# Side loads of the HGRN2 heads and the attention on another queue, in other tiles and in smaller portions

## The chip, the cores and the metric

The kernel runs on one core of a Trainium2 chip. The metric is the device time of one execution in microseconds. An execution is profiled separately, and its trace gives the rows below. Engines: TensorE (PE; its weight loads are PEld), VectorE (DVE), ScalarE (ACT), GpSimd (POOL) and SyncE (SP), which only issues transfers; "q" behind an engine's name is its queue. Each engine takes its instructions in the order of its queue.

## The reference, cut to what matters

A decoder of two layers on x of 1024 rows and 1024 columns, all in float32:

```python
mod = c_act @ ada_w[l] + ada_b[l]                  # 6 vectors of 1024 a layer, 2 more for keys and values
sh1, sc1, g1, sh2, sc2, g2 = jnp.split(mod, 6, axis=-1)
h = modulate(x, sh1, sc1)                          # RMS norm, scale, shift
y = hgrn2_mixer(h, ...)   # layer 0: 8 heads of 128: proj = h @ w_in gives q, f, i, g; chunked scan
y = fox_mixer(h, ...)     # layer 1: 8 heads of attention with forget gates, keys and values shared
x = x + g1 * y
h = modulate(x, sh2, sc2)
u = causal_conv3(h @ w_up)                         # 2 x 2816 channels
x = x + g2 * ((silu(gate) * val) @ w_down)
```

## The kernel before

Each product is of float32 precision: an operand is split into a rounded high part (ScalarE, line 83) and the rest (VectorE, line 84), and three matmuls (lines 102 to 104) add up. Weights come as 512 KB transfers issued by SP into one of two raw buffers (`wraw`); the split goes to one of three buffers (`whl`). The MLP's products are done with block sums of operands and weights, so that seven half-size products stand for eight; for w_down the kernel first forms sums of its rows (`weight_sums`) and stores them in DRAM (`sd`), from where `ffn_down` loads them.

The stages in order are `start` (norm and first modulation), `hgrn` (eight heads), `mixer_out`, `ffn_up`, `ffn_down`, `shared_kv`, `fox` (eight heads of attention), and again `mixer_out`, `ffn_up` and `ffn_down`.

Heads are counted from 0: head 2 is the third. A head of `hgrn` is `forget` (dense product, sigmoid at line 618, cumulative sums, exponentials), `rest` (three dense products for q, i and g), `scan` (transposes, a product masked by VectorE's copy at line 697, the state products at line 710 and the recurrence at line 719) and `outputs`, with `gate` one head later. `gate` puts the head's output in a stream tile. There are eight stream tiles (`x_tile`, pool `xp`); in the heads they are free once x is spilled to DRAM in head 0, and are taken up one by one by the outputs.

Beside the heads runs side work. `ada_plan` makes a list of steps, one for each 128 rows of an adaLN vector's weights: load 512 KB (line 301, GpSimd's queue, one of three buffers `raw`) and multiply and add into `acc` (VectorE, line 305 for the first and 307 for the other seven). When a vector's eight steps are done, `ada_close` sums over partitions with matmuls (line 353). `weight_sums` makes eleven pairs of row blocks of w_down, each with two loads (line 330), one sum and three differences of half rows (lines 331 and 336) and two stores (line 339). For layer 0 a pair is one step of the same list, with the same three buffers, behind the first 48 adaLN steps; 48 more follow it. `ada_step(n)` takes n steps from the list: `SIDE` says how many behind q, behind i and behind the scan. For layer 1 the sums run in `fox`, two steps of 44 at each query block, in stream tiles.

In `ffn_up`, group j makes 128 gate and 128 value channels; `weight_tiles(j)` loads its two raw weights (line 825) into `wraw`, and `weights` splits them and their block sums. `first_groups` does groups 0 and 1 together and begins group 2, while `flush` still makes the operands from the eight stream tiles. The framework sets the order on each queue and the waits when it builds the program; a buffer's next user waits for its last reader.

Of the kernel before, what the change touches and what calls it, by code (L numbers as in the profile page):

```python
# [4 lines left out]
F32 = mybir.dt.float32  # L5
# [8 lines left out]
P = 128  # L14
D = 1024
S = 1024
# [30 lines left out]
ST = 1  # L47
NAT = (5, 0)
KLATE = True
SIDE = (4, 6, 4)  # L50
LATE = 7
FILL = ((1, 1, 1), (2, 0, 2), (2, 0, 2), (0, 2, 3), (2, 0, 2), (2, 1, 4), (0, 0, 1), (2, 0, 2))

# [1 line left out]
class Trunk:  # L55
# [240 lines left out]
    def ada_plan(self, vectors):  # L296

        def block(key, v, one, k, box):
            def step():
                raw = self.adap.tile([P, D], F32, tag="raw", name="ada_raw", bufs=3)  # L300
                self.nc.gpsimd.dma_start(raw, self.ada_w[key][k * P:(k + 1) * P, v * D:(v + 1) * D])
                c = self.cact[:, k:k + 1]
                if k == 0:
                    box.append(self.adap.tile([P, D], F32, tag="acc", name="acc", bufs=1))
                    self.nc.vector.tensor_scalar(out=box[0], in0=raw, scalar1=c, scalar2=None, op0=ALU.mult)
                else:
                    self.nc.vector.scalar_tensor_tensor(out=box[0], in0=raw, scalar=c, in1=box[0],  # L307
                                                        op0=ALU.mult, op1=ALU.add)
                if k == KT - 1:
                    self.ada_open.append((key, v, one, box[0]))  # L310
            return step

        for key, v, one in vectors:
            box = []
            self.ada_todo += [block(key, v, one, k, box) for k in range(KT)]

    def weight_sums(self, l, tiles):

        V, G, down = self.nc.vector, self.nc.gpsimd, self.t["ffn_w_down"][l]

        def pair(i):
            e, o = [], []

            def first():
                for r, raws in ((2 * i, e), (2 * i + 1, o)):
                    raws.append(tiles())
                    G.dma_start(raws[0], down[r * P:(r + 1) * P, :])  # L330
                V.tensor_tensor(out=o[0][:, HALF:D], in0=e[0][:, HALF:D], in1=o[0][:, HALF:D], op=ALU.add)

            def minus(out, a, b, row=None, raws=None):
                def f():
                    (t0, c0), (t1, c1), (t2, c2) = out, a, b
                    V.tensor_tensor(out=t0[0][:, c0:c0 + HALF], in0=t1[0][:, c1:c1 + HALF], in1=t2[0][:, c2:c2 + HALF],
                                    op=ALU.subtract)
                    if raws:
                        G.dma_start(self.sd[l][row * P:(row + 1) * P, :], raws[0])
                return f  # L340

            return [first, minus((e, HALF), (e, 0), (e, HALF)), minus((e, 0), (o, HALF), (e, 0), 2 * i, e),
                    minus((o, 0), (o, 0), (e, 0), 2 * i + 1, o)]

        return [pair(i) for i in range(NFF // 2)]

    def ada_close(self):

        nc = self.nc
        for key, v, one, acc in self.ada_open:  # L350
            ps = self.aux_tile()
            for j in range(KT):
                nc.tensor.matmul(ps[:, j:j + 1], acc[:, j * P:(j + 1) * P], self.ones[:, 0:1], start=True, stop=True)
            s = slice(v * KT, (v + 1) * KT)
            dst, bias = self.mods[key][:, s], self.ada_bias[key][:, s]
            if one:
                nc.vector.scalar_tensor_tensor(out=dst, in0=ps[:, 0:KT], scalar=1.0, in1=bias, op0=ALU.add, op1=ALU.add)
            else:
                nc.vector.tensor_tensor(out=dst, in0=ps[:, 0:KT], in1=bias, op=ALU.add)
        self.ada_open = []  # L360

    def ada_step(self, n):

        todo, self.ada_todo = self.ada_todo[:n], self.ada_todo[n:]
        for step in todo:
            step()
# [220 lines left out]
    def hgrn(self, hs):  # L587
# [3 lines left out]
        with self.work("hg") as wp:  # L591
            def T(tag):
                return wp.tile([P, S], F32, tag=tag, name="hg_" + tag)
# [47 lines left out]
                return a, b, c, d, e  # L641

            def rest(h, a, b, c, d, e, before):
                pq = self.mm_tile()
                w = self.early.pop(0) if self.early else self.w_cols(w_in, h * P)
                for n in range(2):
                    self.dense(pq[:, n * HALF:(n + 1) * HALF], w, hs, n)
                    if n == 0:
                        self.ada_close()
                q = T("q")  # L650
                nc.scalar.activation(q, pq, AF.Silu)
                nc.vector.tensor_tensor(out=e, in0=q, in1=e, op=ALU.mult)
                nc.vector.tensor_tensor(out=q, in0=q, in1=c, op=ALU.mult)
                self.ada_step(SIDE[0])

                pi = self.mm_tile()
                w = self.w_cols(w_in, 2 * D + h * P)
                for n in range(2):
                    self.dense(pi[:, n * HALF:(n + 1) * HALF], w, hs, n)
                    if n == 0:  # L660
                        self.ada_close()
                before()
                vt = T("a")
                nc.scalar.copy(vt, pi)
                self.ada_step(SIDE[1])

                pg = self.mm_tile()
                w = self.w_cols(w_in, 3 * D + h * P)
                for n in range(2):
                    self.dense(pg[:, n * HALF:(n + 1) * HALF], w, hs, n)  # L670
                    if n == 0:
                        self.ada_close()
                sg = T("sg")
                nc.scalar.activation(sg, pg, AF.Silu)
                self.ada_close()

                return b, c, d, e, q, vt, sg
# [90 lines left out]
            f, before = forget(0), lambda: None  # L768
            for h in range(NH):
                b, c, d, e, q, vt, sg = rest(h, *f, before)  # L770
                if h == 0:
                    for n in range(2):
                        self.spill_x(n)
                v, sv = scan(b, c, d, e, q, vt)
                if h == 0:
                    self.conv_setup()
                self.ada_step(SIDE[2])
                if h < NH - 1:
                    f = forget(h + 1)
                before = lambda h=h, on=outputs(q, v, sv), sg=sg: gate(h, on, sg)  # L780
# [34 lines left out]
    def ffn_up(self, l, ops):  # L815


        nc, t, V = self.nc, self.t, self.nc.vector
# [1 line left out]
        Q = KT // 2  # L820

        def weight_tiles(j):
            g, v = (self.wraw.tile([P, S], F32, tag="wraw", name="wraw_t") for _ in range(2))
            for raw, c0 in ((g, j * P), (v, (NFF + j) * P)):
                nc.sync.dma_start(raw.rearrange("p (k m) -> p k m", k=KT),
                                  up[:, c0:c0 + P].rearrange("(k p) m -> p k m", p=P))
            return g, v
# [99 lines left out]
        def first_groups():  # L927
# [14 lines left out]
            gate_right(a)  # L942
            first_gate(b)
            raws = weight_tiles(2)
            do(p7(a))
            do(p4(a))
# [329 lines left out]
    def fox(self, hs):  # L1276
        nc, t = self.nc, self.t
        wq = t["b_w_q"][0]
        V, G = nc.vector, nc.gpsimd
        self.ogf = [None] * NH  # L1280
        with self.work("fx") as wp:
# [36 lines left out]
            def head_sig(s):  # L1318
                s["sg"] = wp.tile([P, S], F32, tag="sg", name="fx_sg")
                with self.tc.high_priority():  # L1320
                    nc.scalar.activation(s["sg"], s["pg"], AF.Sigmoid)
                    self.ln_exp_set()
# [75 lines left out]
            norm()  # L1398
            advance(s, 16)
            head_sig(s)  # L1400
            sums = [f for steps in self.weight_sums(1, lambda: self.x_tile("down_raw")[0]) for f in steps]
            for h in range(NH):
                last = h == NH - 1
                for i in range(KT):
                    if h < 3 or i < 4:
                        for f in sums[:2]:
                            f()
                        sums = sums[2:]
                    ls = logits(s, i)
                    if not last:  # L1410
                        if i == 0:
# [51 lines left out]
    def body(self):  # L1463
        t, mod = self.t, self.mod

        def new():
            return [[None, None] for _ in range(KT)]

        h, hk, h1 = new(), new(), new()
        self.sqacc = [None, None]  # L1470
        self.pending = []
        self.ada_todo, self.ada_open = [], []
        with self.work("ln") as self.lnp, self.work("first") as wp:
            self.start(wp, h)
        self.ada_plan([(0, v, v == 4) for v in (2, 3, 4, 5)] + [("kv", v, v == 1) for v in range(2)])
        self.ada_todo += [lambda steps=steps: [f() for f in steps] for steps in self.weight_sums(0, lambda: self.adap.tile([P, D], F32, tag="raw", name="down_raw", bufs=3))]
        self.ada_plan([(1, v, v in (1, 4)) for v in range(6)])

        def ln(hs, shift, scale1, keep=False):
# [63 lines left out]
```

## Time and profile before

| | |
|---|---|
| median of 3 runs | 2630.34 us (2621.69 to 2631.52) |
| profiled execution | 2626.53 us, span 2624.8 us |
| mean granted TensorE clock | 0.977 |
| busy TensorE, VectorE, ScalarE, GpSimd | 96%, 71%, 46%, 12% of the span |
| moved by DMA | 362.11 MB, mean 138 GB/s |

The span goes from the first to the last instruction. A row of windows has the stretch (us from the span's start), its length, the busy us (and count) of PE, PEld, DVE, ACT and POOL, the granted clock, the mean busy share of the 16 DMA engines, and GB/s; with a line or tile given, the busy us are those of its instructions on the engines that have any. The granted clock is a share of full speed. Busy time of TensorE is modelled, since its matmuls are pipelined. A row of waits names who waited, for whom, for how long in total, how often, and the longest.

### The profile page before, as it was taken

What the parts mean: (1) busy time and instruction counts of PE and PEld (TensorE: products, weight loads), DVE (VectorE), ACT (ScalarE), POOL (GpSimd) and SP (SyncE); (2) the same over time, 40 slices, a digit from 0 to 9 for tenths busy, and PEclk for the clock granted to TensorE, in tenths of its full rate; (3) what the DMA queues carried; (4) which work ended last, traced back from release to release, by engine and by line L of the source; (5) the groups of instructions that cost most, each with busy time, mean ns of one, the idle gap of its engine ahead of it and who ended that gap; (6) DMA issues with size and microseconds to landing.
All of it is one profiled execution on the core that took longest, in us unless ns stands there. A gap on an engine that the chain in (4) does not pass through costs nothing.

```text
span 2624.8 us, 32311 instructions
## 1 busy us (share of the span) xinstructions
PE 2529.3 (96%) x12312; PEld 2089.2 (80%) x12312; DVE 1859.0 (71%) x2703; ACT 1204.2 (46%) x1767; POOL 325.0 (12%) x464
## 2 busy tenths in 40 slices
PE   7999988999999999999999999999998999999999
PEld 5788777778778888878888987888886887887887
DVE  6666656675877878886765367767658777879754
ACT  6333222234544444544645355556545444445442
POOL 3212222211000000000120034323210000000000
PEclk8999998899999999999999999999999999999999
DMA  8653667535122222573343457432511222228423
GB/s 291 193 161 97 209 208 249 161 111 165 37 81 80 82 87 81 177 258 111 125 138 125 149 209 273 148 101 73 165 61 57 80 86 75 81 89 296 137 94 119
DMA packets 298642, 362.11 MB, mean 138 GB/s; under 512 B 14166, under 2 KB 214980, under 8 KB 298486
## 3 DMA queue, kind: packets, MB, share of 16 engines
q1 hardware_dynamic: 271510, 263.30, 30.7%
q0 software_dynamic: 26976, 96.73, 10.7%
q8 instruction: 97, 1.59, 0.2%
q14 instruction: 59, 0.48, 0.1%
HBM read 276.06 MB, written 83.92 MB: 137 GB/s over the span
## 4 chain that ended last, share of the span: by engine, by line
PE 70%; DVE 11%; DMA 8%; issue 6%; ACT 2%; POOL 1%; SPq 0%; POOLq 0%; DVEq 0%; ACTq 0%
PE mm_t L102 12%; PE mm_t L104 12%; PE mm_t L103 12%; PE aux_t L102 10%; PE aux_t L104 10%; PE aux_t L103 10%; DMA ada_raw<-in_ada_w 3%; DMA wraw_t<-in_ffn_w_up 2%; DVE whl_t L84 2%; DMA sd<-down_raw 1%; PE aux_t L1369 1%; DMA down_raw<-in_ffn_w_down 1%; DVE op_t L84 1%; DVE acc L307 1%; ACT whl_t L83 1%
## 5 line engine op out<-in xcount | busy, mean ns | idle before, releaser
L84 DVE TENSOR_TENSOR whl_t<-wraw_t,whl_t 128x1024 fp32r<-128x1024 f32 (+1 forms) x332 | 374.7, 1139 | 124.7 <-ACT whl_t L83 120.8
L83 ACT CAST whl_t<-wraw_t 128x1024 fp32r<-128x1024 f32 (+1 forms) x332 | 320.1, 975 | 281.1 <-DVE wraw_t L842 91.9
L102 PE MATMUL mm_t<-op_t,whl_t 128*128 128x512 f32 x968 | 379.1, 393 | 15.4 <-ACT whl_t L83 11.6
L103 PE MATMUL mm_t<-op_t,whl_t 128*128 128x512 f32 x968 | 378.7, 392 | 1.9 <-DVE op_t L84 1.9
L104 PE MATMUL mm_t<-op_t,whl_t 128*128 128x512 f32 x968 | 377.9, 391 | 0.0
L102 PE MATMUL mm_t<-h_t,whl_t 128*128 128x512 f32 x896 | 365.5, 408 | 0.0
L103 PE MATMUL mm_t<-h_t,whl_t 128*128 128x512 f32 x896 | 356.5, 398 | 1.2 <-DVE h_t L446 0.9
L102 PE MATMUL aux_t<-op_t,whl_t 128*128 128x512 f32 x880 | 349.7, 398 | 7.2 <-ACT whl_t L83 4.1
L104 PE MATMUL mm_t<-h_t,whl_t 128*128 128x512 f32 x896 | 356.4, 398 | 0.0
L103 PE MATMUL aux_t<-op_t,whl_t 128*128 128x512 f32 x880 | 344.4, 391 | 1.2 <-DVE op_t L84 1.1
L104 PE MATMUL aux_t<-op_t,whl_t 128*128 128x512 f32 x880 | 342.9, 391 | 2.4 <-DVE whl_t L84 2.4
L102 PEld LDWEIGHTS mm_t<-op_t,whl_t 128*128 128x128 f32 x968 | 182.6, 189 | 58.8 <-ACT whl_t L83 13.3
L103 PEld LDWEIGHTS mm_t<-op_t,whl_t 128*128 128x128 f32 x968 | 182.8, 189 | 41.3 <-DVE op_t L84 4.2
L104 PEld LDWEIGHTS mm_t<-op_t,whl_t 128*128 128x128 f32 x968 | 182.5, 189 | 39.3 <-DVE whl_t L84 1.4
L102 PEld LDWEIGHTS aux_t<-op_t,whl_t 128*128 128x128 f32 x880 | 165.7, 188 | 54.5 <-ACT whl_t L83 15.5
L104 PEld LDWEIGHTS mm_t<-h_t,whl_t 128*128 128x128 f32 x896 | 171.9, 192 | 38.0 <-issue 0.5
L103 PEld LDWEIGHTS mm_t<-h_t,whl_t 128*128 128x128 f32 x896 | 172.5, 193 | 34.7 <-DVE h_t L446 1.3
L102 PEld LDWEIGHTS mm_t<-h_t,whl_t 128*128 128x128 f32 x896 | 172.3, 192 | 33.7 <-issue 2.1
L104 PEld LDWEIGHTS aux_t<-op_t,whl_t 128*128 128x128 f32 x880 | 165.3, 188 | 38.8 <-DVE whl_t L84 3.3
L103 PEld LDWEIGHTS aux_t<-op_t,whl_t 128*128 128x128 f32 x880 | 165.7, 188 | 37.0 <-DVE op_t L84 2.9
L403 POOL TENSOR_TENSOR sqacc<-sqacc,sq 128x512 f32<-128x512 f32 x29 | 43.2, 1489 | 765.6 <-ACT sq L402 765.2
L307 DVE SCALAR_TENSOR_TENSOR acc<-ada_raw,cact,acc 128x1024 f32<-128x1024 f32 x84 | 107.6, 1281 | 38.0 <-DMA ada_raw<-in_ada_w 33.5
(317 smaller groups left out, 4395.9 us busy)
## 6 DMA issues: line engine op xcount, KB each, us to landing
wraw_t<-in_ffn_w_up SPq DMA_DIRECT2D x88, 512.0 KB, 3.8
ada_raw<-in_ada_w POOLq DMA_DIRECT2D x80, 512.0 KB, 4.9
down_raw<-in_ffn_w_down POOLq DMA_DIRECT2D x44, 512.0 KB, 5.5
sd<-down_raw POOLq DMA_DIRECT2D x44, 512.0 KB, 4.1
gd<-u SPq DMA_DIRECT2D x44, 512.0 KB, 2.6
graw<-gd SPq DMA_DIRECT2D x44, 512.0 KB, 6.4
wraw_t<-sd SPq DMA_DIRECT2D x40, 512.0 KB, 3.4
wraw_t<-in_a_w_in SPq DMA_DIRECT2D x32, 512.0 KB, 5.2
```

Of the source, the lines that this page charges most:

```text
L83: self.nc.scalar.copy(hi, src)
L84: self.nc.vector.tensor_tensor(out=lo, in0=src, in1=hi.bitcast(F32), op=ALU.subtract)
L102: mm(out, wh, xh, start=start, stop=False, skip_group_check=onto)
L103: mm(out, wh, xl, start=False, stop=False, skip_group_check=onto)
L104: mm(out, wl, xh, start=False, stop=stop, skip_group_check=onto)
L307: self.nc.vector.scalar_tensor_tensor(out=box[0], in0=raw, scalar=c, in1=box[0], op0=ALU.mult, op1=ALU.add)
L403: (nc.gpsimd if k in SQPOOL else nc.vector).tensor_tensor(out=self.sqacc[n], in0=self.sqacc[n], in1=sq, op=ALU.add)
L1369: nc.tensor.transpose(pp[:, b * P:(b + 1) * P], ls[:, kb * P:(kb + 1) * P], self.ident)
```

## The change

- The transfers of the adaLN steps and of the sums (loads and stores) are issued by SP instead of GpSimd.
- The sums of layer 0 leave the list of adaLN steps: `sum_step(4)` takes one pair's four steps, once in head 0 behind the scan, and in heads 1 to 5 behind q and behind i. Their tiles are stream tiles.
- While `ada_spare` is set (from the end of head 0 until the scan of head 5), every second adaLN load has a stream tile instead of one of the three buffers.
- `SIDE` has four portions: 2 steps at the start of `rest`, 3 behind q, 4 behind i and 3 behind the scan, 12 a head for 96 steps.
- In `ffn_up`, the raw weights of group 2 go to two stream tiles instead of `wraw`, in both layers.

```diff
@@ -47,7 +47,7 @@
 ST = 1
 NAT = (5, 0)
 KLATE = True
-SIDE = (4, 6, 4)
+SIDE = (3, 4, 2, 3)
 LATE = 7
 FILL = ((1, 1, 1), (2, 0, 2), (2, 0, 2), (0, 2, 3), (2, 0, 2), (2, 1, 4), (0, 0, 1), (2, 0, 2))
 
@@ -297,8 +297,12 @@
 
         def block(key, v, one, k, box):
             def step():
-                raw = self.adap.tile([P, D], F32, tag="raw", name="ada_raw", bufs=3)
-                self.nc.gpsimd.dma_start(raw, self.ada_w[key][k * P:(k + 1) * P, v * D:(v + 1) * D])
+                self.ada_turn += 1
+                if self.ada_spare and self.ada_turn % 2:
+                    raw = self.x_tile("ada_raw")[0]
+                else:
+                    raw = self.adap.tile([P, D], F32, tag="raw", name="ada_raw", bufs=3)
+                self.nc.sync.dma_start(raw, self.ada_w[key][k * P:(k + 1) * P, v * D:(v + 1) * D])
                 c = self.cact[:, k:k + 1]
                 if k == 0:
                     box.append(self.adap.tile([P, D], F32, tag="acc", name="acc", bufs=1))
@@ -319,7 +323,7 @@
 
 
 
-        V, G, down = self.nc.vector, self.nc.gpsimd, self.t["ffn_w_down"][l]
+        V, G, down = self.nc.vector, self.nc.sync, self.t["ffn_w_down"][l]
 
         def pair(i):
             e, o = [], []
@@ -358,6 +362,12 @@
             else:
                 nc.vector.tensor_tensor(out=dst, in0=ps[:, 0:KT], in1=bias, op=ALU.add)
         self.ada_open = []
+
+    def sum_step(self, n=4):
+
+        todo, self.sums = self.sums[:n], self.sums[n:]
+        for step in todo:
+            step()
 
     def ada_step(self, n):
 
@@ -641,6 +651,7 @@
                 return a, b, c, d, e
 
             def rest(h, a, b, c, d, e, before):
+                self.ada_step(SIDE[2])
                 pq = self.mm_tile()
                 w = self.early.pop(0) if self.early else self.w_cols(w_in, h * P)
                 for n in range(2):
@@ -652,6 +663,8 @@
                 nc.vector.tensor_tensor(out=e, in0=q, in1=e, op=ALU.mult)
                 nc.vector.tensor_tensor(out=q, in0=q, in1=c, op=ALU.mult)
                 self.ada_step(SIDE[0])
+                if 0 < h < 6:
+                    self.sum_step()
 
                 pi = self.mm_tile()
                 w = self.w_cols(w_in, 2 * D + h * P)
@@ -663,6 +676,8 @@
                 vt = T("a")
                 nc.scalar.copy(vt, pi)
                 self.ada_step(SIDE[1])
+                if 0 < h < 6:
+                    self.sum_step()
 
                 pg = self.mm_tile()
                 w = self.w_cols(w_in, 3 * D + h * P)
@@ -771,10 +786,14 @@
                 if h == 0:
                     for n in range(2):
                         self.spill_x(n)
+                    self.ada_spare = True
+                if h == 5:
+                    self.ada_spare = False
                 v, sv = scan(b, c, d, e, q, vt)
                 if h == 0:
                     self.conv_setup()
-                self.ada_step(SIDE[2])
+                    self.sum_step()
+                self.ada_step(SIDE[3])
                 if h < NH - 1:
                     f = forget(h + 1)
                 before = lambda h=h, on=outputs(q, v, sv), sg=sg: gate(h, on, sg)
@@ -820,7 +839,8 @@
         Q = KT // 2
 
         def weight_tiles(j):
-            g, v = (self.wraw.tile([P, S], F32, tag="wraw", name="wraw_t") for _ in range(2))
+            g, v = (self.x_tile("uraw")[0] if j == 2 else self.wraw.tile([P, S], F32, tag="wraw", name="wraw_t")
+                    for _ in range(2))
             for raw, c0 in ((g, j * P), (v, (NFF + j) * P)):
                 nc.sync.dma_start(raw.rearrange("p (k m) -> p k m", k=KT),
                                   up[:, c0:c0 + P].rearrange("(k p) m -> p k m", p=P))
@@ -1398,14 +1418,12 @@
             norm()
             advance(s, 16)
             head_sig(s)
-            sums = [f for steps in self.weight_sums(1, lambda: self.x_tile("down_raw")[0]) for f in steps]
+            self.sums = [f for steps in self.weight_sums(1, lambda: self.x_tile("down_raw")[0]) for f in steps]
             for h in range(NH):
                 last = h == NH - 1
                 for i in range(KT):
                     if h < 3 or i < 4:
-                        for f in sums[:2]:
-                            f()
-                        sums = sums[2:]
+                        self.sum_step(2)
                     ls = logits(s, i)
                     if not last:
                         if i == 0:
@@ -1469,11 +1487,11 @@
         h, hk, h1 = new(), new(), new()
         self.sqacc = [None, None]
         self.pending = []
-        self.ada_todo, self.ada_open = [], []
+        self.ada_todo, self.ada_open, self.ada_turn, self.ada_spare = [], [], 0, False
         with self.work("ln") as self.lnp, self.work("first") as wp:
             self.start(wp, h)
         self.ada_plan([(0, v, v == 4) for v in (2, 3, 4, 5)] + [("kv", v, v == 1) for v in range(2)])
-        self.ada_todo += [lambda steps=steps: [f() for f in steps] for steps in self.weight_sums(0, lambda: self.adap.tile([P, D], F32, tag="raw", name="down_raw", bufs=3))]
+        self.sums = [f for steps in self.weight_sums(0, lambda: self.x_tile("down_raw")[0]) for f in steps]
         self.ada_plan([(1, v, v in (1, 4)) for v in range(6)])
 
         def ln(hs, shift, scale1, keep=False):
```

## Rows read from the trace of the kernel before

**Rows 1.** The page: busy us, share of the span and instructions of each engine.

```profile
PE 2529.3 (96%) x12312; PEld 2089.2 (80%) x12312; DVE 1859.0 (71%) x2703; ACT 1204.2 (46%) x1767; POOL 325.0 (12%) x464
```

**Rows 2.** Windows from sigmoid to sigmoid: heads 0 to 6 together, 1, 2, 5, 6.

```profile
67.61:531.02 463.41, 431.42 (x2280) 356.12 (x2279) 303.51 (x390) 143.59 (x157) 100.67 (x164) 0.92 0.57 184
...
127.21:192.69 65.48, 63.26 (x352) 52.50 (x352) 44.33 (x55) 19.81 (x22) 11.97 (x20) 0.95 0.51 161
192.69:249.82 57.13, 57.13 (x328) 47.88 (x328) 35.07 (x45) 19.81 (x23) 10.20 (x12) 1.00 0.35 111
...
382.12:455.67 73.55, 63.96 (x313) 53.82 (x312) 46.61 (x49) 21.19 (x23) 17.49 (x32) 0.89 0.72 235
455.67:531.02 75.35, 72.00 (x375) 56.68 (x375) 53.80 (x73) 21.66 (x24) 15.69 (x26) 0.86 0.54 172
```

**Rows 3.** Waits of TensorE in 67.61:531.02, longest in total first.

```profile
PE aux_t L353 <- DVE acc L307: 15.2, 4, 8.3
PE aux_t L710 <- DVE st L697: 13.8, 7, 6.7
```

**Rows 4.** Waits of VectorE in 60:600.

```profile
DVE down_raw L331 <- DMA down_raw<-in_ffn_w_down: 41.2, 10, 7.2
DVE acc L307 <- DMA ada_raw<-in_ada_w: 33.5, 30, 4.2
```

**Rows 5.** Timeline of GpSimd: start, us, instruction, idle before it and its releaser.

```profile
287.76 0.54 POOL L339 DMA_DIRECT2D sd<-down_raw x1 [7.86 <-DVE down_raw L336]
...
291.82 0.53 POOL L330 DMA_DIRECT2D down_raw<-in_ffn_w_down x1 [2.80 <-DMA sd<-down_raw]
```

**Rows 6.** Windows: line 307 (heads 2, 5), line 305 (head 2), tile down_raw (VectorE, GpSimd).

```profile
192.69:249.82 57.13, 8.98 (x7) 1.00 0.35 111
...
382.12:455.67 73.55, 19.25 (x15) 0.89 0.72 235
...
192.69:249.82 57.13, 0.74 (x1) 1.00 0.35 111
...
249.82:407.00 157.18, 29.82 (x44) 23.18 (x43) 0.95 0.56 191
```

**Rows 7.** Windows: MLP of layer 0 and 1, attention, the most DMA.

```profile
720.00:750.00 30.00, 24.71 (x100) 19.79 (x99) 23.10 (x26) 14.03 (x17) 0.00 (x0) 0.89 0.27 87
1995.00:2025.00 30.00, 26.11 (x106) 20.94 (x105) 27.32 (x31) 14.74 (x17) 0.00 (x0) 0.89 0.26 83
...
1530.00:1680.00 150.00, 143.40 (x753) 122.03 (x753) 114.06 (x285) 79.31 (x163) 62.22 (x109) 0.97 0.72 245
...
2400.00:2425.00 25.00, 24.42 (x107) 19.71 (x106) 25.00 (x38) 9.59 (x15) 0.00 (x0) 1.00 0.99 372
```

**Rows 8.** Waits of SP's queue in 60:600; timelines of SP and ScalarE, head 2.

```profile
SPq L91 <- DVE whl_t L84: 350.9, 24, 37.9
...
224.88 0.37 SPq L91 DMA_DIRECT2D wraw_t<-in_a_w_in  x1
...
234.55 1.09 ACT L83 CAST whl_t<-wraw_t 128x1024 fp32r<-128x1024 f32 x1
```

**Rows 9.** Timelines of VectorE, SP, ScalarE and TensorE, first MLP groups, layer 0.

```profile
709.40 1.28 DVE L84 TENSOR_TENSOR op_t<-x_r,op_t 128x512 fp32r<-128x512 f32 x2
...
714.27 1.21 DVE L84 TENSOR_TENSOR whl_t<-wraw_t,whl_t 128x1024 fp32r<-128x1024 f32 x1
...
725.91 0.37 SPq L825 DMA_DIRECT2D wraw_t<-in_ffn_w_up  x1
...
730.12 1.04 ACT L83 CAST whl_t<-wraw_t 128x1024 fp32r<-128x1024 f32 x1 [2.08 <-DMA wraw_t<-in_ffn_w_up]
...
731.22 0.80 PE L102 MATMUL mm_t<-op_t,whl_t 128*128 128x512 f32 x1 [5.29 <-ACT whl_t L83]
```

**Rows 10.** Waits of GpSimd in 1500:1700.

```profile
POOL sd L339 <- DVE down_raw L336: 22.0, 7, 10.2
```

**Rows 11.** The page's DMA issues: line, queue, count, KB each, median us to landing.

```profile
ada_raw<-in_ada_w POOLq DMA_DIRECT2D x80, 512.0 KB, 4.9
```

## The prediction

> **What bounds the kernel now.** I read the share of busy time first: TensorE is busy nearly all of the span [rows 1], so a change off TensorE can win only TensorE's idle time, and time in which it works at the lower of its two clocks (1.2 instead of 2.4 GHz). Where those lie, the windows by stage tell. The change touches three places.
>
> First, the eight HGRN2 heads. I cut the trace at the sigmoid of each head's forget gate, so that one window is one head's period. Seven periods take 463.41 us; TensorE is busy for 431.42 of these, at a mean granted clock of 0.92 [rows 2]. The reader is to see how unequal the heads are. The third takes 57.13 us, all of them busy, at a clock of 1.00: with eight side steps on VectorE it is a quiet head. The sixth and seventh take 73.55 and 75.35 at 0.89 and 0.86. Seven quiet heads would take 7 x 57.13 = 399.9, so 63.5 us are lost: 463.41 - 431.42 = 32.0 idle, and the rest goes with the clock, which by its mean would cost 0.08 x 463.4 = 37 (the two overlap a little and the clock is rounded).
>
> Second, the list of waits says what TensorE stands for in those periods: the closing matmul of an adaLN vector for VectorE's accumulator, and the state product of the scan for VectorE's masked copy [rows 3]. Both are VectorE late, not VectorE full: it is busy 303.5 of the 463.4 us [rows 2]. VectorE itself waits 41.2 us for rows of w_down and 33.5 us for rows of adaLN weights [rows 4]. Its queue is in order, so the scan stands behind these.
>
> Third, GpSimd's timeline shows why rows come late: a store of sums waits for VectorE (7.86 us), the next load for such a store to land (2.80), and VectorE again for that load [rows 5]. All eleven pairs (44 VectorE steps) pass three shared buffers one after another inside 249.8 to 407 us, and the layer 1 vectors, planned behind them, crowd into the last heads (15 accumulations at line 307 in the sixth, 7 in the quiet one) [rows 6].
>
> Outside the heads, the windows around the third and fourth MLP groups hold 30 - 24.71 = 5.3 and 30 - 26.11 = 3.9 us of idle TensorE at a clock of 0.89, and the first attention heads 150 - 143.40 = 6.6 at 0.97 [rows 7].
>
> **Part 1: adaLN loads and sums of the heads.** VectorE's work stays: 96 accumulating steps and 44 steps on half rows. What changes is when and behind what. A plan of 4, 6 and 4 steps a head becomes 2, 3, 4 and 3, so no portion exceeds the three reserved buffers by more than one, and in heads 1 to 5 every second load has a stream tile instead. The sums leave that plan: two pairs in each of heads 1 to 5, one in head 0, in stream tiles. In head 5, the fullest, five stream tiles hold gated outputs, so three are left, enough for a pair and one load; in head 1 seven are left, enough for two pairs. So a pair need no longer wait for the one before, and the 41.2 us of VectorE waits lose their cause. GpSimd loses its side transfers in the heads; its norm work no longer stands behind them.
>
> What each head has to hold: a quiet head's VectorE has 35.07 us, of which 8.98 + 0.74 are eight accumulating steps, so 25.4 are its own; twelve steps cost 12/8 x 9.72 = 14.6 and eight sum steps 8/44 x 29.82 = 5.4 [rows 2, 6]. That is 45.4 of 57.13, 80%, in heads 1 to 5 and 40 in the others. It fits, but with in-order work in front of the scan: the second head, with 44.3 us of VectorE, took 65.48 [rows 2]. Bounds for a head are thus 57.13 (nothing lost) and the second head's 65.48. Since the new heads have more buffers than that one had, I stay nearer to the lower: 3 us over quiet for five heads, 1.5 for the other two in the seven periods: 399.9 + 15 + 3 = 417.9. Gain: 463.4 - 417.9 = 45.5 us; bounds 63.5 and 463.4 - 7 x 65.48 = 5.
>
> **Part 2: SP's queue.** The loads pass to a queue that stands still most of the time: 350.9 us in 24 waits for a weight buffer that VectorE's split frees [rows 8]. A side load written behind such a weight load stands with it, and a weight load behind a side load waits for an accumulation. The weight loads have room: one is issued at 224.88 and first read at 234.55 [rows 8]; with 4.9 us to land, as the adaLN rows need [rows 11], 4.8 us of delay cost nothing. Issuing costs SP 0.37 us each [rows 9], for 20 more per head 7 us of 57, while SP only waits. I take 0; the bound is the second rival. HBM traffic per full head is 12 + 4 + 4.4 + 4.4 transfers of 0.52 MB = 13.0 MB, in 57 us 228 GB/s, against 235 in the sixth head, and 372 where the kernel moves most [rows 2, 7].
>
> The Trainium skill speaks against this part: "DMA: Bandwidth & Descriptors", section "Issuing engines are not separate DMA queues", says that DMAs issued from several engines run on the same 16 DMA engines and that the choice saves only issue time. By that rule alone the change of queue brings nothing and part 1 would have to come from the buffers and portions; the rows agree so far, since what they show late is the issue, not the transfer.
>
> **Part 3: third MLP group in stream tiles.** Now the fourth group's first load is issued at 725.91, when the third group's split frees its buffer; it lands, the cast starts at 730.12 and TensorE has stood 5.29 us at 731.22 [rows 9]; in layer 1 the window lacks 3.9. With groups 0 and 1 in the two reserved buffers and group 2 elsewhere, the fourth group's loads can go as soon as the second group's weights are split. With the clock (0.11 x 30 = 3.3 each) the two places hold 8.6 + 7.2 = 15.8 us. What is late next is the third group itself: it now waits for stream tiles, whose last operands are split at 709.40 to 710.7. From issue to cast 4.2 us as above, a cast of 1.04 and a split of 1.21 give 717.1, against 715.5 now (714.27 + 1.21) [rows 9]: 1.6 us late, and two issues of 0.37 on top, 2.4. Twice that: net gain 11; bounds 15.8, and 0 if the tiles come later still.
>
> **Part 4: attention.** The 44 steps and their pace are the same; GpSimd's bias tiles no longer queue behind stores that wait for VectorE (22.0 us in 1500:1700) [rows 10]. The place holds 6.6 + 0.03 x 150 = 11.1 us; since SP there also waits for nfk, k and v, whose order I cannot see, half of it: 6; bounds 11, and -6 if a store that waits for VectorE holds the next head's loads for as long.
>
> **Sum.** 45.5 + 11 + 6 = 62 off the profiled execution's 2626.5 (span 2624.8) gives 2564. That execution is 3.8 below the median of the three runs, within their spread of 9.8; half of the difference on top: 2566.
>
> **Rivals.**
>
> *A, half of it.* Heads 1 to 5 end like the second head, because VectorE at 80% in front of the scan takes over as what ends last: 5 x 8.35 = 42 instead of 15 us over quiet, and 3 for the rest. Gain in the heads 18.5, with MLP and attention between 0 and 17: 2590 to 2608. For it: the waits on the masked copy already hold 13.8 us [rows 3]. Against: they fall in the heads in which VectorE waited for w_down.
>
> *B, slower: SP's order.* Side loads stand behind weight loads that wait for a split, which stands on VectorE behind the accumulation that needs the side load: then each such meeting shows a full landing, 4.9 us [rows 11], on VectorE. It decides from 9 us a head on (63.5 / 7), two meetings a head. With three, 14.7 us a head, I price the head as the sixth now: 16.4 over quiet, 7 x 16.4 = 115 instead of 63.5, so 51 longer; less 11 in the MLP, 2666. For it: SP's waits of up to 37.9 us. Against: each load now has more buffers to go ahead in.
>
> *C, no change.* The sixteen DMA engines, not the order, set the landings (0.72 busy in the sixth head); the lateness moves from buffers to transfers and heads 1 to 6 stay at 66: 463, within 12 of before with the MLP's gain. This is the skill's rule of part 2 taken as the bound. Against: 372 GB/s elsewhere.
>
> **Chances.** Forecast (2535 to 2590) 0.60, A 0.22, B 0.10, C 0.08. All gains at their bounds give 2626.5 - 63.5 - 15.8 - 11 = 2536, which is the lower end; the upper, 2608, takes in A and leaves out most of B and C. A run of this kernel can tell about 0.5% from no change (2617 to 2643): faster 0.84, same 0.07, slower 0.09.
>
> **What would show it.** Right: head periods of 57 to 62 us with a clock near 1, VectorE's waits for w_down gone, sums spread over heads 1 to 5, no stall of TensorE at the fourth MLP group. Wrong: waits of TensorE for weight casts in the heads (B), DMA share above 0.85 there with landings of 8 us and more (C), or waits on the masked copy of over 3 us a head (A).

## The result, and the profile after

The changed kernel takes 2565.05 us (median of 4 runs, 2562.96 to 2566.35) against 2626.02 for the kernel before in the same comparison: a ratio of 0.9767 with a 95% interval of 0.974 to 0.9793. I had forecast 2566 in 2536 to 2608. The two profiled spans are 2624.8 and 2564.3 us. Cut at the same events of both traces, the 60.5 us between them lie here:

| stretch | before | after | gain | forecast |
|---|---|---|---|---|
| seven head periods | 463.4 | 419.0 | 44.4 | 45.5 |
| layer 0, first x store to first load of the down product | 480.2 | 475.7 | 4.5 | MLPs |
| attention, first to last sigmoid of the output gate | 301.0 | 295.2 | 5.8 | 6 |
| layer 1, last x store to last load of the down product | 460.9 | 455.1 | 5.8 | 11 for both MLPs |

The page's first section, and the windows from sigmoid to sigmoid (all seven, then heads 0 to 6; columns as in [rows 2]):

```profile
PE 2494.9 (97%) x12312; PEld 2063.1 (80%) x12312; DVE 1859.6 (73%) x2703; ACT 1200.7 (47%) x1765; POOL 239.5 (9%) x280
```

```profile
67.46:486.45 418.99, 406.93 (x2280) 339.53 (x2279) 304.52 (x392) 140.34 (x154) 36.34 (x29) 0.98 0.61 205
67.46:121.92 54.46, 50.80 (x260) 42.05 (x258) 44.62 (x57) 21.62 (x22) 1.68 (x3) 0.97 0.91 303
121.92:185.35 63.43, 60.42 (x342) 50.19 (x343) 40.71 (x55) 19.70 (x23) 5.41 (x6) 0.97 0.55 191
185.35:249.98 64.63, 62.41 (x344) 52.03 (x344) 48.64 (x62) 19.80 (x22) 5.85 (x4) 0.95 0.56 194
249.98:307.11 57.13, 57.13 (x328) 47.88 (x328) 40.47 (x53) 19.81 (x23) 5.85 (x4) 1.00 0.67 222
307.11:368.03 60.92, 59.54 (x344) 49.67 (x344) 48.42 (x62) 19.80 (x23) 5.85 (x4) 1.00 0.60 206
368.03:425.15 57.12, 57.12 (x328) 47.87 (x328) 37.71 (x49) 19.80 (x22) 5.86 (x4) 1.00 0.49 159
425.15:486.45 61.30, 59.49 (x344) 49.82 (x344) 43.95 (x54) 19.81 (x22) 5.85 (x4) 1.00 0.53 172
```

The work is the same (2280 matmuls in the periods, as in [rows 2]; VectorE 304.5 against 303.5 us). TensorE's idle time there fell from 32.0 to 12.1 us, 19.9 of the 44.4. The other 24.5 are busy time, 431.4 to 406.9 for the same matmuls: the granted clock rose from 0.92 to 0.98. More than half of the gain is thus clock. That it goes with the waits can be seen where one wait stands alone: where head 1 begins TensorE stands 4.16 us up to 124.93, for the convolution's columns. Windows of 5 us there:

```profile
120.00:125.00 5.00, 0.84 (x5) 0.41 (x4) 0.00 (x0) 3.59 (x3) 0.00 (x0) 0.94 0.70 229
125.00:130.00 5.00, 5.00 (x17) 3.75 (x17) 1.01 (x2) 1.99 (x2) 1.36 (x2) 0.71 0.02 5
130.00:135.00 5.00, 5.00 (x49) 3.83 (x50) 4.97 (x5) 0.00 (x0) 0.00 (x0) 1.00 0.00 0
```

In the 5 us behind the wait TensorE works at a mean granted clock of 0.71, and then at 1.00 again.

Head 3, with 40.5 us of VectorE, is as short as the quiet head; the last two of the seven, 73.55 and 75.35 before, are at 57.12 and 61.30. The windows do not all hold the same work (260 matmuls in head 0, 328 to 344 in the others), so seven times the quiet head, 399.9 us, is a bound for the sum and not for each head.

TensorE's and VectorE's waits in the periods, against [rows 3] and [rows 4]:

```profile
PE aux_t L725 <- DVE st L712: 4.3, 3, 2.5
PE aux_t L176 <- DMA st_ca<-in_ffn_conv_w: 4.2, 1, 4.2
PE aux_t L357 <- DVE acc L311: 3.5, 2, 2.2
```

```profile
DVE acc L311 <- DMA ada_raw<-in_ada_w: 13.2, 9, 3.6
...
DVE down_raw L335 <- DMA down_raw<-in_ffn_w_down: 2.2, 1, 2.2
```

The wait for rows of w_down fell from 41.2 to 2.2 us, and that for the closing matmul from 15.2 to 3.5. In the MLP, timelines of SP, VectorE and TensorE, layer 0, and windows at the same place in both layers, against [rows 9] and [rows 7]:

```profile
660.86 1.01 SPq L845 DMA_DIRECT2D uraw<-in_ffn_w_up  x2
...
664.37 1.28 DVE L84 TENSOR_TENSOR op_t<-x_r,op_t 128x512 fp32r<-128x512 f32 x2
...
669.22 1.21 DVE L84 TENSOR_TENSOR whl_t<-uraw,whl_t 128x1024 fp32r<-128x1024 f32 x1
...
685.30 0.50 PE L102 MATMUL mm_t<-op_t,whl_t 128*128 128x512 f32 x1 [0.79 <-ACT gate L982]
```

```profile
674.00:704.00 30.00, 29.21 (x128) 23.60 (x127) 26.26 (x30) 16.83 (x20) 0.00 (x0) 1.00 0.15 53
1944.00:1974.00 30.00, 29.21 (x129) 23.60 (x128) 26.25 (x30) 17.37 (x20) 0.00 (x0) 1.00 0.15 53
```

At the fourth group 0.79 us of idle are left of 5.3 and 3.9, at full clock. The third group's loads went out at 660.86, some 4 us before the last stream tile was read at 664.4 to 665.7, so they had the tiles that come free first. Its first split follows the last operand's split (664.37) by 4.85 us, as before (709.40 and 714.27), so it did not come late.

### The profile page after: what moved, and what is told of

Its sections match the earlier page's. It is cut to its first block, busy times and chain, and to the rows that moved or that the text cites. A ratio compares the mean times of both kernels' runs of the same rounds, so it can differ in the third digit from the quotient of the medians.

```text
span 2564.3 us, 32233 instructions
## 1 busy us (share of the span) xinstructions
PE 2494.9 (97%) x12312; PEld 2063.1 (80%) x12312; DVE 1859.6 (73%) x2703; ACT 1200.7 (47%) x1765; POOL 239.5 (9%) x280
## 4 chain that ended last, share of the span: by engine, by line
PE 73%; DVE 12%; DMA 4%; ACT 3%; issue 2%; POOL 1%; SPq 0%; DVEq 0%; ACTq 0%; POOLq 0%
PE mm_t L102 13%; PE mm_t L104 13%; PE mm_t L103 13%; PE aux_t L102 10%; PE aux_t L104 10%; PE aux_t L103 10%; DVE whl_t L84 2%; DMA wraw_t<-in_ffn_w_up 2%; PE aux_t L1389 1%; DVE acc L311 1%; DVE op_t L84 1%; DMA ada_raw<-in_ada_w 1%; ACT whl_t L83 1%; DVE u L921 1%; ACT u L918 1%
## 5 line engine op out<-in xcount | busy, mean ns | idle before, releaser
L84 DVE TENSOR_TENSOR whl_t<-wraw_t,whl_t 128x1024 fp32r<-128x1024 f32 (+1 forms) x324 | 366.5, 1143 | 114.2 <-ACT whl_t L83 111.7
L83 ACT CAST whl_t<-wraw_t 128x1024 fp32r<-128x1024 f32 (+1 forms) x324 | 312.2, 976 | 257.8 <-DVE wraw_t L862 97.5
L104 PEld LDWEIGHTS mm_t<-h_t,whl_t 128*128 128x128 f32 x896 | 170.2, 190 | 36.5 <-issue 0.2
L103 PEld LDWEIGHTS mm_t<-h_t,whl_t 128*128 128x128 f32 x896 | 170.7, 190 | 34.8 <-DVE h_t L456 2.2
L102 PEld LDWEIGHTS mm_t<-h_t,whl_t 128*128 128x128 f32 x896 | 170.5, 190 | 33.7 <-issue 1.6
L83 ACT CAST op_t<-graw 128x512 fp32r<-128x512 f32 x132 | 80.7, 619 | 84.1 <-PE mm_t L104 45.1
L311 DVE SCALAR_TENSOR_TENSOR acc<-ada_raw,cact,acc 128x1024 f32<-128x1024 f32 x84 | 107.6, 1281 | 15.2 <-DMA ada_raw<-in_ada_w 14.2
```

Of the source, the lines that this page charges most:

```text
L83: self.nc.scalar.copy(hi, src)
L84: self.nc.vector.tensor_tensor(out=lo, in0=src, in1=hi.bitcast(F32), op=ALU.subtract)
L102: mm(out, wh, xh, start=start, stop=False, skip_group_check=onto)
L103: mm(out, wh, xl, start=False, stop=False, skip_group_check=onto)
L104: mm(out, wl, xh, start=False, stop=stop, skip_group_check=onto)
```

## The experiments

First the two kernels against themselves. The heads of *e1* are those of the kernel before, and of *e8* those of the changed one; their seven periods came out at 460.9 (463.4) and 417.7 (419.0). So the sum of the seven agrees within 2.6 us between two profiles of the same heads. Single heads do not: the last of the seven took 67.9 us in *e1* and 75.4 before. The ratio in the table is to the kernel before in the same comparison; times are in us.

| run | time | ratio (95%) | seven periods |
|---|---|---|---|
| e1 third group alone | 2614.47 | 0.9949 (0.9931 to 0.9966) | 460.9 |
| e2 changed, all on GpSimd | 2574.85 | 0.9805 (0.9788 to 0.9823) | 422.5 |
| e3 before, all on SP | 2589.73 | 0.9859 (0.9843 to 0.9876) | 427.5 |
| e8 changed, attention on GpSimd | 2568.05 | 0.9773 (0.9752 to 0.9793) | 417.7 |
| e5 changed, three buffers | 2586.60 | 0.9857 (0.984 to 0.9873) | 443.6 |
| e7 changed, pairs in heads 3, 4 | 2578.78 | 0.9829 (0.9812 to 0.9846) | 432.1 |
| e10 before, norm on VectorE | 2611.49 | 0.9947 (0.9927 to 0.9968) | 444.0 |
| e12 before, sums on SP | 2606.67 | 0.9933 (0.9915 to 0.9951) | 444.3 |
| e4 changed, no tiles for adaLN | 2559.33 | 0.9745 (0.9723 to 0.9766) | 411.7 |
| e6 changed, 4-6-4 portions | 2565.19 | 0.9766 (0.9742 to 0.9789) | 416.9 |
| e9 changed, columns in head 6 | 2562.50 | 0.9755 (0.9734 to 0.9777) | 413.1 |
| e13 before, SP, pairs' tiles | 2585.86 | 0.9846 (0.982 to 0.9872) | 434.2 |

**e1, the third group alone.** 
```diff
-  g, v = (self.wraw.tile([P, S], F32, tag="wraw", name="wraw_t") for _ in range(2))
+  g, v = (self.x_tile("uraw")[0] if j == 2 else self.wraw.tile([P, S], F32, tag="wraw", name="wraw_t")
+          for _ in range(2))
```

> The kernel before with the third MLP group's raw weights in stream tiles and nothing else. My theory: this part acts alone, the waits of TensorE at the fourth group fall from 5.3 and 3.9 us to under 1.5, the heads stay at 463 us, total 10 us less, ratio 0.996. Rival: the group only moves its wait to the third group or to the stage's end, and the MLP's gain in the changed kernel came from the earlier stages: ratio 1.000.

As my theory had it: 10 us less. The waits for casts at the fourth group, 5.3 and 3.9 us, are 1.1 us in layer 0 and gone in layer 1. Over all profiled kernels with this edit, the loop from the first store of channels to the first load of the down product in layer 0 took 355.0 us (ten) against 358.6 (four without it), and in layer 1, last x store to last store of channels, 443.2 against 449.4: 3.6 and 6.2.

**e2 and e3, the queue.**

```diff
# e2, in the changed kernel                 # e3, in the kernel before: the reverse
-  self.nc.sync.dma_start(raw, self.ada_w...)
+  self.nc.gpsimd.dma_start(raw, self.ada_w...)
-  V, G, down = self.nc.vector, self.nc.sync, ...
+  V, G, down = self.nc.vector, self.nc.gpsimd, ...
```

> The changed kernel with its side loads and stores issued by GpSimd again; portions, order and stream tiles stay. My theory: the heads live from portions and buffers, so their seven periods stay within 419 to 427 us and only the attention gives back its 6: 2565 + 6 to 14, ratio 0.979 to 0.982. Rival (the queue makes the gain, because GpSimd's norm work and its stores held the loads up): seven periods of 440 us and more, ratio 0.988 or above.

> The kernel before with its side loads and stores issued by SP and nothing else. My theory: the pairs of w_down still pass three shared buffers one by one, so the seven periods stay at 455 to 470 us; the attention gains 6; ratio 0.995 to 1.000. Rival queue: periods near 425, ratio 0.98. Rival order of SP (side loads and weight loads hold each other up): periods above 480, ratio above 1.005.

e2 went as my theory had it: without the queue the heads give back 3.5 us, little more than two profiles differ by. e3 did not: the queue alone, with the old list and three shared buffers, takes 36 us off the heads. Its windows of the seven periods and VectorE's waits there:

```profile
65.79:493.25 427.46, 414.37 (x2269) 342.59 (x2267) 302.11 (x386) 143.29 (x157) 28.96 (x29) 0.97 0.61 200
```

```profile
DVE acc L307 <- DMA ada_raw<-in_ada_w: 22.0, 20, 2.7
DVE down_raw L331 <- DMA down_raw<-in_ffn_w_down: 20.6, 7, 6.1
```

So two remedies, each good for 36 to 41 us alone, give 44 together: they cure the same lateness. The last two heads are still 70.7 and 69.6 in e3 (57.1 and 61.3 in the changed kernel). The whole kernel gains less than these places: in e3 heads and attention give 42 us and the profiled span is 36.7 shorter, in e12 (below) 26 and 20.3. Several other stages are 1 to 2 us longer there, and why is open.

That transfers issued by GpSimd are slower in themselves is not borne out: with the queue alone changed, rows of w_down land in 5.6 us against 5.5 and stores of sums in 3.9 against 4.1 (medians).

**e10 and e12, what GpSimd's queue held up.**

```diff
# e10 (an inverse stands for the inverse root)
-  nc.gpsimd.tensor_scalar(out=ss[:, s4], ...)
+  nc.vector.tensor_scalar(out=ss[:, s4], ...)
-  nc.gpsimd.tensor_tensor(out=ss[:, s4], ..., op=ALU.pow)
+  nc.vector.reciprocal(ss[:, s4], ss[:, s4])
# e12
-  V, G, down = self.nc.vector, self.nc.gpsimd, ...
+  V, G, down = self.nc.vector, self.nc.sync, ...
```

> The kernel before with the small norm steps of the heads' outputs on VectorE instead of GpSimd (an inverse stands for the inverse root there), so that GpSimd's loads and stores stand behind no norm step. If the norm steps, for which GpSimd waits 101.8 us in the heads, are what held the side loads up: periods of 445 us or less, ratio 0.993 or below. If it is the chain of pairs and buffers: periods of 458 to 468, ratio 0.998 to 1.002.

> The kernel before with only the loads and stores of w_down issued by SP, in the heads and in the attention; adaLN rows stay on GpSimd and everything on three buffers. If stores that wait for VectorE in GpSimd's queue held up what stood behind them: heads 3 to 6 give 15 to 25 us, the attention 6, ratio 0.988 to 0.992. If the queue acts through the adaLN rows: heads 3 to 6 as before, ratio 0.997.

In the heads both came out as the queue would have it; the whole times stayed above the ratios that I had given (0.9947 against 0.993, 0.9933 against 0.992). The seven periods give 19.4 us with the norm steps on VectorE, and 19.1 with the sums on SP (18.4 of these in heads 3 to 6, and 6.9 more in the attention). Neither touches an adaLN load. VectorE's waits in the periods, two lines of the kernel before, two of e10 and one of e12:

```profile
DVE acc L307 <- DMA ada_raw<-in_ada_w: 31.8, 29, 4.2
...
DVE hg_on L750 <- POOL hg_ss L749: 7.6, 8, 1.2
```

```profile
DVE down_raw L331 <- DMA down_raw<-in_ffn_w_down: 37.2, 10, 7.3
DVE acc L307 <- DMA ada_raw<-in_ada_w: 29.8, 38, 4.4
```

```profile
DVE down_raw L331 <- DMA down_raw<-in_ffn_w_down: 19.5, 6, 6.4
```

e12 speaks for the queue plainly: the wait for rows of w_down falls from 41.2 to 19.5. e10 does so less: these rows come hardly earlier (41.2 to 37.2, and adaLN 31.8 to 29.8 in the same windows), while 7.6 us in which VectorE waited for GpSimd's norm steps are gone, since the steps are now its own. How much of e10's 19.4 is GpSimd's queue is therefore open. What is shown is that loads and stores of the sums and adaLN loads, each waiting for VectorE at another time, stood behind one another in one in-order queue: taking the sums out gives 19, and e3, which leaves the norm steps alone there, 36. One reservation: the framework lays out the other engines' queues anew for each kernel, so some VectorE steps stand elsewhere too, and what this alone gives was not separated.

**e8, the attention's queue.**

```diff
-  V, G, down = self.nc.vector, self.nc.sync, ...
+  V, G, down = self.nc.vector, (self.nc.gpsimd if l else self.nc.sync), ...
```

> The changed kernel with the attention's loads and stores of w_down alone issued by GpSimd again. My theory: the attention gives back its 6 us because bias tiles stand again behind stores, all else stays: 2571, ratio 0.979. Rival: the attention's gain was one of placement, not of the queue: 2565, ratio 0.977.

The stretch of the table above is 301.7 us, against 295.2 with SP. In the five kernels that issue on GpSimd there it averages 300.3 (297.6 to 301.7), in nine that issue on SP 295.5 (294.1 to 297.0): the queue gives 4.8 us. The whole time of e8 is unclear at that size. TensorE's wait there for VectorE's split of pt goes and comes with the queue (before, changed kernel, e8):

```profile
PE aux_t L1369 <- DVE pt L84: 6.2, 2, 3.3
PE aux_t L1389 <- DVE pt L84: 1.6, 2, 0.8
PE aux_t L1389 <- DVE pt L84: 6.1, 2, 3.1
```

**e5, e4, e13 and e7: tiles and list.**

```diff
# e4 and e5
-  self.ada_spare = True
+  self.ada_spare = False
# e5 also
-  self.weight_sums(0, lambda: self.x_tile("down_raw")[0])
+  self.weight_sums(0, lambda: self.adap.tile([P, D], F32, tag="raw", name="down_raw", bufs=3))
# e7, at both places behind q and i; no pair in head 0
-  if 0 < h < 6: self.sum_step()
+  if h in (3, 4): self.sum_step(12)
# e13: kernel before with SP, pairs in x_tile, third group in x_tile
```

> The changed kernel without stream tiles for the side work of the heads: adaLN rows and rows of w_down share the three buffers again, but the queue (SP), the portions and the spread of the pairs over heads 0 to 5 stay. If the queue and the spread suffice: seven periods of 419 to 428 us, ratio 0.977 to 0.981. If the tiles are what counts, as my prediction had it: a pair waits for the stores of the one before and for adaLN rows, periods of 440 us and more, ratio 0.985 or above.

> The changed kernel without stream tiles for adaLN rows; the pairs of w_down keep theirs. If the pairs' tiles are the part that counts, since the three shared buffers then belong to adaLN rows alone and portions of 2 to 4 fit them: seven periods of 419 to 426 us, ratio 0.976 to 0.980. If adaLN rows need the extra tiles: periods of 435 us and more, ratio 0.983 or above.

> The kernel before with the queue of the change (SP), stream tiles for the pairs of w_down and the third group in stream tiles, but the old list and portions: the pairs still stand together in heads 3 and 4, 14 steps a head. If queue and tiles are all: seven periods of 419 to 426 us, ratio 0.977 to 0.979. If the list counts: heads 5 and 6 stay at 69 to 71 us, as with the queue alone, because layer 1's vectors still stand behind the pairs, periods of 427 us and more, ratio 0.981 or above.

> The changed kernel with all eleven pairs in heads 3 and 4, behind q and behind i, in stream tiles and on SP. If the tiles undo the chain of pairs wherever they stand: seven periods of 419 to 428 us, ratio 0.977 to 0.981. If the spread counts: heads 3 and 4 take 66 us and more each, periods of 435 us and more, ratio 0.983 or above.

e5 says that the new order needs the tiles: on SP, it takes 443.6 us with three buffers, 16 more than the old order (e3). VectorE's waits and TensorE's longest in e5's periods:

```profile
DVE acc L311 <- DMA ada_raw<-in_ada_w: 30.7, 20, 5.5
DVE down_raw L335 <- DMA down_raw<-in_ffn_w_down: 22.6, 7, 5.4
```

```profile
PE aux_t L725 <- DVE st L712: 16.4, 6, 5.7
```

e4 says which tiles: those of the pairs. With them, and adaLN rows on their three buffers, the periods fall to 411.7, below the changed kernel's 419.0 and below the 419 to 426 that I expected. So the spare tiles for every second adaLN load give nothing here; the kernel with them is 7 us longer (6 against e8's profile of the same heads). Against the changed kernel the difference lies in heads 0 to 2, 175.4 us in e4 (its windows below) against 182.5; e8's same heads took 178.4:

```profile
66.88:125.81 58.93, 52.79 (x267) 43.22 (x266) 44.94 (x58) 21.63 (x22) 2.71 (x5) 0.97 0.87 280
125.81:183.31 57.50, 57.50 (x336) 47.89 (x336) 40.06 (x54) 19.82 (x23) 3.38 (x4) 1.00 0.55 183
183.31:242.28 58.97, 58.97 (x344) 49.66 (x343) 46.12 (x57) 19.80 (x23) 5.85 (x4) 1.00 0.64 211
```

With spare tiles, head 0 moves 303 GB/s and is shorter (54.46 us against 58.93), but heads 1 and 2 then run at 0.97 and 0.95 with idle time; without, they are quiet. That the tiles alone cost this is not shown: head 1's one listed wait of TensorE is the 4.2 us for the convolution's columns, loaded in head 0. In e9, which keeps the spare tiles and moves that load to head 6, heads 0 to 2 take 171.1 us, and all seven 413.1, which is e4's within what two profiles differ by:

```profile
67.14:238.26 171.12, 168.07 (x940) 140.65 (x939) 133.28 (x170) 61.25 (x67) 11.81 (x8) 0.99 0.70 237
```

VectorE waits longer for side rows in e4 (16.2 and 18.8 us) than in the changed kernel (2.2 and 13.2), and the periods are shorter. TensorE's waits for VectorE's masked copy are 3.5 us in e4 and 4.3 in the changed kernel, so little of VectorE's waiting reached TensorE.

e13 and e7 say that the list counts once queue and tiles are there: e13 is 22.5 us above e4, which has the same tiles, and e7 13 above the changed kernel. The four kernels on SP without spare tiles, side by side (seven periods):

| on SP | pairs together in the list | pairs spread |
|---|---|---|
| three buffers for all | 427.5 (e3) | 443.6 (e5) |
| tiles for the pairs | 434.2 (e13) | 411.7 (e4) |

On SP, either part alone makes the heads longer, by 7 and 16 us; both together make them 16 shorter. (The portions differ between the columns too.)

The loss is not where I expected it in e13 (heads 5 and 6 take 56.0 and 63.1), nor in e7 (heads 3 and 4 take 57.1 and 60.4, where I expected 66 and more): with the pairs together, e13's head 4 is long, and e7's head 5:

```profile
297.37:381.92 84.55, 72.04 (x346) 55.61 (x346) 52.93 (x74) 21.53 (x24) 5.47 (x8) 0.82 0.76 261
```

```profile
359.23:435.16 75.93, 61.13 (x328) 49.90 (x328) 44.95 (x53) 21.66 (x24) 5.80 (x4) 0.87 0.48 150
```

In e7, TensorE stands for weight casts there, which it never does in the heads of the changed kernel (timeline of TensorE; then the landing of the weight loads of 340 to 382 us, to which SP came right behind the last stores of pairs and among six adaLN loads; 5.1 us is the changed kernel's median):

```profile
366.64 0.79 PE L102 MATMUL mm_t<-h_t,whl_t 128*128 128x512 f32 x1 [4.04 <-ACT whl_t L83]
373.68 0.80 PE L102 MATMUL mm_t<-h_t,whl_t 128*128 128x512 f32 x1 [5.82 <-ACT whl_t L83]
379.85 0.79 PE L104 MATMUL mm_t<-h_t,whl_t 128*128 128x512 f32 x1 [4.95 <-DVE whl_t L84]
```

```profile
DMA to landing us min/median/max: 4.2/7.6/11.0
```

This looks like the price of my rival B. e13's long head has such waits as well, 3.8 and 2.2 us. It is not shown to be SP's order alone: VectorE also waits 4.0 us for an adaLN row there and the casts stand behind that head's exponentials on ScalarE.

**e6 and e9, portions and the convolution's columns.**

```diff
# e6
-SIDE = (3, 4, 2, 3)
+SIDE = (4, 6, 0, 4)
# e9
-  if h == 0:
+  if h == 6:
       self.conv_setup()
+  if h == 0:
       self.sum_step()
```

> The changed kernel with portions of 4 behind q, 6 behind i and 4 behind the scan (14 a head, none at the head's start). If the small portions count: 6 steps pass the three buffers and a few tiles in a row, VectorE stands for them, seven periods of 428 us and more, ratio 0.981 or above. If tiles and queue are enough: 419 to 426, ratio 0.977 to 0.979.

> The changed kernel with the load and turn of the convolution's columns in head 6 instead of head 0, where TensorE waits 4.2 us for one of these loads while the DMA engines are at their busiest (share 0.91). If that wait and the clock it costs go: 4 to 8 us less than the changed kernel, 2557 to 2561, ratio 0.974 to 0.9755. If the wait goes along with the load: 2565, ratio 0.977.

With the spare tiles in place the portions do not count (416.9, within what two profiles differ by), though 14 steps a head instead of 12 were asked for. e9's periods fall by 5.9 and the wait of 4.2 us at line 176 is gone, but the whole time against the changed kernel's is within the intervals: inconclusive. Its window of all seven periods:

```profile
67.14:480.22 413.08, 406.53 (x2271) 339.85 (x2270) 304.82 (x391) 140.47 (x155) 37.95 (x29) 0.98 0.62 208
```

The fastest version is e4. Its runs (2557.23 to 2560.97) lie below all of the changed kernel's, in another comparison; the two intervals overlap, so its lead of some 0.2% is likely, not certain. e4 with e9's edit was not run.

## Why the prediction was right, and where it was not

**Total and terms.** Heads 45.5 forecast and 44.4 measured, attention 6 and 5.8, MLPs 11 and 10.3 (4.5 + 5.8). The bound set by the quiet head held for the sum: no kernel's seven periods came below 411.7, against 399.9. Of the single heads, heads 1 and 2 took 63.4 and 64.6 us at 0.97 and 0.95, outside the 57 to 62 and the clock near 1 that I had named as signs.

The closeness in the heads is in part luck. The 3 us over quiet for each full head was a choice between 0 and 8.35, and its reason, more buffers, is half wrong (part 1). Without the queue, which I put at 0, the same list and tiles take 422.5 us (e2), and without the spare tiles, which I held for a help, they take 411.7 (e4); my 417.9 lies between.

**Part 1, right in the mechanism, wrong in one edit.** The chain of pairs through three buffers was a cause, and tiles for the pairs cure it where the pairs are spread (e4 against e5: 32 us, with adaLN rows on their three buffers in both). With the old list they do not: e13 is 7 us above e3. The small portions and the spare tiles, which I counted as help, give nothing (e6 and e4).

**Part 2, the step that failed.** "I take 0" for the queue. From the kernel before, the queue alone takes 36 us off the heads (e3), and I had read the cause in GpSimd's timeline [rows 5] without pricing it: its side transfers stood behind stores that wait for VectorE. It comes out nearly 0 only as the last of the edits (422.5 to 419.0, e2). Two cures of one lateness do not add; my sum held because I had bounded the heads by what a quiet head takes, not by adding cures.

The rule of the Trainium skill that I had weighed ("DMA: Bandwidth & Descriptors", section "Issuing engines are not separate DMA queues": issuing from several engines at once saves only the time of issuing) does not cover this case. The trace agrees that transfers got no faster: adaLN rows land in 5.7 us from SP in the changed kernel against 4.9 [rows 11], and rows of w_down in 5.6 against 5.5 where the queue alone changed (e3). What the queue saved was what its instructions waited behind.

One slip in the traffic, on which nothing rests: two pairs a head are 4 loads and 4 stores, not 4.4 each, so a full head moves 24 transfers, 220 GB/s in 57.13 us; head 3 moved 222.

**Part 3, right, one term too large.** The third group's 2.4 us did not come: its tiles were free by 660.86, as the framework took those read first. But the clock gave back less than I read from the means: 7.6 us of the 10.3 are idle time that went (5.29 + 3.89 to twice 0.79), so 2.7 are left for the clock and all else, in place of 6.6.

**Part 4, right** in size, and the queue is the cause (e8). That it acts through the bias tiles is argued: TensorE's wait for VectorE's split of pt comes back with GpSimd's queue, but the steps between were not followed.

**Rivals.** A did not come: heads 1 to 5 took 303.2 us together, 17.6 over quiet where I had forecast 15 and A 42, and the waits on the masked copy are 4.3 us in all. C did not: head 0 runs the DMA engines at 0.91 and 303 GB/s, up from 0.66 and 205, and took 54.46 us, down from 59.60. B did not in the changed kernel; e7 shows a stall of its kind.

## What to carry to other kernels

Price a stretch by its quietest repetition in the same trace, idle and clock together; here that bound held for the sum although I had the shares of the edits wrong. Before a change with several parts is credited to one of them, undo each and do each alone: where both a part alone and the rest without it give most of the gain, they cure the same wait. Parts can also need each other: on SP, tiles for the pairs and spreading them each cost time alone and gained 16 us together. An in-order queue that carries work of several kinds, each waiting for another engine, can hold all of them up while it is itself little busy (GpSimd was 12% busy, and moving its transfers to SP took 36 us of 463 off the heads).

## What the runs showed of the hardware that I had not expected

Waits for loads on VectorE were no measure of loss here: 35 us of them in e4 beside 411.7, 15 beside 419.0. And the clock gave back more than the idle time did: in the heads 24.5 us of busy time against 19.9 of waits, for the same matmuls.
